# Experts of a product-key layer: the look-up of the chosen ones in PSUM, some splits on GpSimd, the gate through DRAM, weights moved by 96 bytes

## The chip, the cores and the metric

One core of a Trainium2 chip runs the whole kernel. Its engines are TensorE (PE, with PEld for its weight loads), VectorE (DVE), ScalarE (ACT), GpSimd (POOL) and SyncE (SP), which issues all DMAs. The metric is the device time of one execution in microseconds; the median over the runs is given.

## The reference

Two blocks of a transformer follow each other on 256 tokens of width 1024: two layers with feed-forward parts, convolution, pooling and neighbourhood attention, then one layer with retention, sparse attention and a mixture of experts. Only the experts and what frames them matter here:

```python
q = (hblk @ w_q).reshape(B, TB, 8, 2, 128)
s = jnp.einsum('btphd,phnd->btphn', q, subkeys)
v, i = lax.top_k(s, 16)
cand = (v[..., 0, :, None] + v[..., 1, None, :]).reshape(B, TB, 8, 256)
cidx = (i[..., 0, :, None] * 128 + i[..., 1, None, :]).reshape(B, TB, 8, 256)
tv, tj = lax.top_k(cand, 16)
eidx = jnp.take_along_axis(cidx, tj, axis=-1)
w = jax.nn.softmax(tv, axis=-1)
a = jax.nn.gelu(jnp.einsum('btd,btpkd->btpk', hblk, w_down[eidx]))
y = jnp.einsum('btpk,btpkd->btd', w * a, w_up[eidx])
x = x + ga2[:, None, :] * y      # then rms_norm(x, g_norm_final)
```

There are 128 x 128 = 16384 experts. Each token chooses 16 for each of 8 heads: the best 16 of 128 first keys, the best 16 of 128 second keys, and the best 16 of their 256 sums.

## The kernel before, in words

All matrices are float32. To keep that precision a weight `w` is split into a high part (`activation Copy` to float32r on ACT, L252) and the rest (`w - high`, on POOL at L254 or on DVE at L256); a product is then three matmuls (`mm3`, L298 to L300: high by high, high by low, low by high).

`Stream` (L232 to L285) feeds the weights in a fixed order of units of 128 x 1024. A unit is loaded by SP into a raw buffer, split into one of four buffers, and used. Splits run three units ahead of the use. The split buffers of the experts' stage are `hl0`, `hl1` and two parts of Hh and Hl called `c0`, `c1` (second half of each, L1153 to L1155); the raw ones are `raw0`, `raw1` and two parts of X. A pad of 56 floats (`gap0`) ahead of `hl0` puts hl at 224 bytes past a multiple of 256; units that `wide` names are put 8 floats further on:

```python
if hl.shape[-1] == SPLIT:
    o = 8 if wide(label) else 0
    hl = hl[:, o:o + 2048].rearrange("p (a n) -> p a n", a=2)
```

`c0` and `c1` begin at 2048 floats of Hh and Hl, at a multiple of 256 bytes, for all units alike.

The last third of the kernel is `peer`. It has these stages:

- 16 query units `wpq` and the key scores (L1611 to L1620), for 256 tokens in two halves of 128.
- All 16384 experts are computed for all tokens: `expert(e)` is one row of 128 experts, 24 matmuls of 256 columns with the weights `wdn` e as the stationary operand. Gelu on ACT (L1593) puts the 128 x 256 result into slot e. While the first rows run on PE, DVE computes the top-k (`topk`): sorts (L1750 to L1758), the sums (L1766), more sorts, and then the look-up, which finds the keys of the chosen pairs by comparing with a table of 0 to 15 (`iota`), multiplying and adding up (L1788, L1791, L1793, 2048 elements each, four times). Its scratch is `cand` in SBUF, its table is in SBUF, and DVE runs in program order, as every engine does.
- The result is transposed (L1648) into SELT. From then on, between the matmuls of the further rows, each token gets a 128 x 128 matrix of its weights: two one-hots on DVE (L1670 for four tokens, L1674 for one) and a product on PE (L1682). Four tokens fill one bank of PSUM, in turn banks 5, 6, 7; `place` multiplies them into the finished slots on DVE (L1691) and copies them to the others on ACT (L1693). The table is copied to bank 4 first (L1656). Experts rotate over banks 0 to 3 here and over six banks before.
- `finish`: for e from 0 to 127 slot e is split (`prep`, L324 and L325, two rows ahead, rows 0 and 1 after the last expert) and is the stationary operand for the weights `wup` e: 12 matmuls of 512 columns (L1841) added up in banks 4 to 7. After e = 32 `ends` loads the residual and the final norm's weights, and spreads the gate over the partitions: eight diagonal matrices on DVE (L1831), eight products with a matrix of ones on PE (L1832), two copies (L1833). The tail gates, adds, normalises and stores.

Of the kernel before, what the change touches and what calls it, by code (L numbers as in the profile page):

```python
# [189 lines left out]
class Stream:  # L190
# [45 lines left out]
    def split(self, upto):  # L236
        nc = self.nc
        while self.done < min(upto, len(self.units)):
            i = self.done
            self.load(i + 1)  # L240
            label, _, n, split = self.units[i]
            if i not in self.raws:
                return
            if split:
                hl = self.buf(i, 2)
                if hl is None:
                    return
                if hl.shape[-1] == SPLIT:
                    o = 8 if wide(label) else 0
                    hl = hl[:, o:o + 2048].rearrange("p (a n) -> p a n", a=2)  # L250
                raw = self.raws.pop(i)
                nc.scalar.activation(hl[:, 0, :n], raw[:, :n], AF.Copy)  # L252
                if i in (1, 2) or label[0] == "wdn" or (label[0] == "win2f" and label[1] > 7 or label[0] == "win2r" or label[:2] == ("winf", 1) and label[2] in (0, 4, 11) or label[0] == "wout2" and label[1] < 5):
                    nc.gpsimd.tensor_tensor(hl[:, 1, :n], raw[:, :n], hl[:, 0, :n].bitcast(F32), OP.subtract)  # L254
                else:
                    nc.vector.tensor_tensor(hl[:, 1, :n], raw[:, :n], hl[:, 0, :n].bitcast(F32), OP.subtract)  # L256
                self.hls[i] = hl
            self.done += 1
# [28 lines left out]
class Build:  # L287
# [40 lines left out]
    def run(self):  # L328
        nc, tc, ctx, I = self.nc, self.tc, self.ctx, self.I
        ctx.enter_context(tc.manual_schedule())  # L330
        base = ctx.enter_context(tc.tile_pool(name="base", bufs=1))
        psum = ctx.enter_context(tc.tile_pool(name="psum", bufs=1, space=bass.MemoryType.PSUM))
        self.bank = [psum.tile([P, 512], F32, name=f"bank{b}") for b in range(8)]
        self.X = base.tile([P, 2, KD, S], F32, name="X")
        self.Hh = base.tile([P, 2, KD, S], F32R, name="Hh")
        self.Hl = base.tile([P, 2, KD, S], F32R, name="Hl")
        raw = [base.tile([P, 1024], F32, name=f"raw{j}") for j in range(2)]
        base.tile([P, 56], F32, name="gap0")
        hl = [base.tile([P, SPLIT], F32R, name=f"hl{j}") for j in range(2)]
        self.con1 = base.tile([P, N1], F32, name="con1")  # L340
        self.mad2 = base.tile([P, 48], F32, name="mad2")
        self.half = base.tile([P, 4], F32, name="halfc")
        base.tile([P, 16], F32, name="gap1")
        self.sm = ctx.enter_context(tc.tile_pool(name="small", bufs=2))

        self.W = Stream(nc, 5, 3)
        self.plan()
        fb = ExitStack()
        fbp = fb.enter_context(tc.tile_pool(name="fb", bufs=1))
        self.G = fbp.tile([P, 2, 8, 512], F32R, name="G")  # L350
        self.Gh, self.Gl = self.G[:, 0], self.G[:, 1]
        self.raws = [("r0", raw[0]), ("r1", raw[1]), ("r2", fbp.tile([P, 1024], F32, name="raw2"))]
        fbp.tile([P, 56], F32, name="gap2")
        self.hls = [("h0", hl[0]), ("h1", hl[1])]
        self.hls += [(f"h{j}", fbp.tile([P, SPLIT], F32R, name=f"hl{j}")) for j in (2, 3)]
        W = self.W
        W.ring(0, self.raws, self.hls)

        cc = self.np_cc = base.tile([P, KD, 2], F32, name="cc")
        nc.sync.dma_start(cc.rearrange("p k c -> p (k c)"), I["cvt"])  # L360
        nc.sync.dma_start(self.con1, I["con1"])
        nc.vector.memset(self.half, -0.5)
        self.C = {k: self.con1[:, o:o + n] for k, (o, n) in OFF1.items()}
        self.ring = [0, 1, 2, 3, 4, 5]

        self.np = fb.enter_context(tc.tile_pool(name="norm", bufs=2))
        self.gn = self.np.tile([P, 72], F32, name="gn", bufs=1)
        nc.sync.dma_start(self.gn, I["gn"])
        with tc.tile_pool(name="mod", bufs=2) as mp:
            with tc.tile_pool(name="first", bufs=8) as self.fm:  # L370
                self.mods_setup(mp)
            self.first_block()
            self.need(2, 5)
        self.second_mix()
        self.peer(fb)
# [768 lines left out]
    def second_mix(self):  # L1144
        nc, tc, I, W = self.nc, self.tc, self.I, self.W
        T = S
        with tc.tile_pool(name="mix2", bufs=1) as p:
# [2 lines left out]
            W.ring(W.done, self.raws + [("xr", Xc[:, 1024:])], self.hls + [("hx", p.tile([P, SPLIT], F32R, name="hx"))])  # L1150
            W.ring(W.index("win2r", 0, 0), self.raws, self.hls + [("hx", W.rings[-1][2][-1][1])])
            Xf = self.X.rearrange("p a k t -> p a (k t)")
            Hf = [H[:, 1].rearrange("p k t -> p (k t)").rearrange("p (a n) -> p a n", a=2) for H in (self.Hh, self.Hl)]  # L1153
            W.ring(W.index("wpq", 4), self.raws[:2] + [("x0", Xf[:, 1, :1024]), ("x1", Xf[:, 1, 1024:])],
                   self.hls[:2] + [(f"c{j}", Hf[j]) for j in range(2)])  # L1155
            con = p.tile([P, N2 - P], F32, name="con2")
# [402 lines left out]
    def peer(self, fb):  # L1559
        nc, tc, I, W = self.nc, self.tc, self.I, self.W  # L1560
        T = S
        ident = self.C["ident"]
        xd = tc.dram_tile([P, 2 * D], F32, name="xd")
        Xf = self.X.rearrange("p a k t -> p a (k t)")
        fb.close()
        bs = self.pq
        pp = self.ctx.enter_context(tc.tile_pool(name="pp", bufs=1))
        SELT = Xf[:, 0, :768].rearrange("p (a t) -> p a t", a=3)
        con = pp.tile([P, P], F32, name="iota")
        self.SA = self.ctx.enter_context(tc.tile_pool(name="slota", bufs=1)).tile([P, NSA * S], F32, name="slotA")  # L1570
        slots = [self.SA[:, e * S:(e + 1) * S] for e in range(NSA)]
        built = [0]
# [26 lines left out]
        with tc.tile_pool(name="topk", bufs=1) as p:  # L1599
# [27 lines left out]
                scores(f, bs.pop(0))  # L1627
            nc.sync.dma_start(xd, xt.rearrange("p t d -> p (t d)"))
            nc.sync.dma_start(con, I["con2"][:, OFF2["iota"][0]:OFF2["iota"][0] + P])
            top = self.topk(p, con, SC, SEL)  # L1630
            e = 0
            spare = 0.0
            while spare is not None and e < NSA - 4:
# [17 lines left out]
                self.dump("SELT", Xf[:, 0, :1024])  # L1651
        slotB = self.ctx.enter_context(tc.tile_pool(name="slots", bufs=1)).tile([P, (P - 1 - NSA) * S], F32, name="slotB")
        slots += [slotB[:, j * S:(j + 1) * S] for j in range(P - 1 - NSA)] + [Xf[:, 0, 1792:2048]]
        self.ring = [0, 1, 2, 3]
        io = self.bank[4][:, :P]
        nc.vector.tensor_copy(io, con)  # L1656
        wb = [5, 6, 7]
        SAv = self.SA.rearrange("p (e t) -> p e t", t=S)
        SCv = Xf[:, 0:1, 1792:2048]
        SBv = slotB.rearrange("p (e t) -> p e t", t=S)  # L1660
# [16 lines left out]
        def weight(t):  # L1677
            if t >= T:
                return
            oh = ohs.pop(t)  # L1680
            o = self.bank[wb[t // 4 % 3]][:, t % 4 * P:(t % 4 + 1) * P]
            nc.tensor.matmul(o, firsts[t // 4][:, t % 4], oh, start=True, stop=True)  # L1682

        def place(g, e):

            bv = self.bank[wb[g % 3]].rearrange("p (t e) -> p e t", e=P)
            ts = slice(4 * g, 4 * g + 4)
            for v, e0, e1 in ((SAv, 0, NSA), (SBv, NSA, P - 1), (SCv, P - 1, P)):
                m = min(max(e, e0), e1)
                if m > e0:  # L1690
                    nc.vector.tensor_tensor(v[:, :m - e0, ts], v[:, :m - e0, ts], bv[:, e0:m], OP.mult)  # L1691
                if m < e1:
                    nc.scalar.activation(v[:, m - e0:, ts], bv[:, m:e1], AF.Copy)  # L1693
            built[0] = 4 * g + 4
# [16 lines left out]
                tok[0] += 1  # L1711

        rest = None
        while e < P or tok[0] < T:
            g0 = tok[0] // 4
            if e < P:
# [12 lines left out]
            if e < P:  # L1729
                rest = gelu(e, o)  # L1730
                e += 1
        if rest:
            rest()

        self.finish(slots, xd, pp)

    def topk(self, p, iota, SC, SEL):

# [43 lines left out]
        io = iota[:, :16].unsqueeze(1).broadcast_to((P, P, 16))  # L1782
        for a in range(2):
            for t in range(2):
                eq = cand[t]
                iv = i16f[t].rearrange("p (h a) n -> p h a n", a=2)
                flat = eq.rearrange("p h k n -> p (h k) n")
                nc.vector.tensor_tensor(flat, abf[t][:, a].rearrange("p h k -> p (h k)").unsqueeze(2).broadcast_to((P, P, 16)),  # L1788
# [14 lines left out]
            nc.vector.tensor_tensor(w[t], w[t], b16(ss[t][:, 1].unsqueeze(2)), OP.mult)  # L1803
        yield 1.2

    def finish(self, slots, xd, pp):
        nc, I, W = self.nc, self.I, self.W
        acc = [[self.bank[4 + 2 * t + c] for c in range(2)] for t in range(2)]
        cs = {}
        Hx = self.Hh[:, 0].rearrange("p k t -> p (k t)")  # L1810
        Hf4 = [Hx[:, j * 512:(j + 1) * 512] for j in range(4)]

        def prep(e):
            c = Hf4[e % 4].rearrange("p (a t) -> p a t", a=2)
            self.split2((c[:, 0], c[:, 1]), slots[e])
            cs[e] = c

        ga = self.mod(2, 0, 5)
        SA = self.SA
        xt = SA[:, :2048].rearrange("p (t d) -> p t d", t=2)  # L1820
        gf, gab, tmp = [SA[:, j * 1024:(j + 1) * 1024] for j in range(2, 5)]
        dgs = [SA[:, 5120 + j * P:5120 + (j + 1) * P] for j in range(4)]

        def ends():

            nc.sync.dma_start(SA[:, :2048], xd)
            nc.sync.dma_start(gf, I["gfin"].broadcast_to((P, D)))
            for n in range(2):
                b = self.bank[n]
                for j in range(4):  # L1830
                    nc.vector.tensor_scalar(dgs[j], self.C["ident"], ga[:, 4 * n + j:4 * n + j + 1], None, op0=OP.mult)  # L1831
                    nc.tensor.matmul(b[:, j * P:(j + 1) * P], self.C["ones"], dgs[j], start=True, stop=True)  # L1832
                nc.vector.tensor_copy(gab[:, n * 512:(n + 1) * 512], b)  # L1833

        def up(e, u, t, c, outer=False):
            ts = slice(t * P, (t + 1) * P)
# [5 lines left out]
                                 start=e == 0 and a + b == 0, stop=e == P - 1 and a == 1)  # L1842

        LATE = 4
        prep(0)
        prep(1)
        for e in range(P - LATE):
            u = W.next("wup", e)
# [44 lines left out]
```

## Time and profile before

| | us |
|---|---|
| median of 3 runs | 2723.25 (2722.06 to 2727.45) |
| profiled execution | 2724.21 |
| its span | 2722.3 |
| PE busy | 2639.4 (97%) |
| PEld, DVE, ACT, POOL busy | 2312.6, 1759.6, 1102.2, 507.7 |
| HBM read | 446.35 MB, 165 GB/s |

The span runs from the first to the last instruction; the execution's own time is 1.9 us more. Matmuls overlap, so the busy time of PE says where it stands still, and the distance between starts says how fast it is.

### The profile page before, as it was taken

To read this page: it belongs to the slowest core of one execution; us is meant where nothing else is said; L and a number is where in the kernel's file an instruction comes from. 1 tells how busy PE (TensorE), PEld (TensorE's weight loads), DVE (VectorE), ACT (ScalarE), POOL (GpSimd) and SP (SyncE) were. 2 spreads that over 40 slices of the span, in tenths; PEclk is the share of its full clock that TensorE was granted. 3 is DMA by queue.
4 is the path that set the end of the run, shared out by engine and by line. 5 is a ranking of instruction groups with operands and counts; after the bars stand their busy time and mean duration, and the time that the engine had idled before them with its cause. 6 is when DMAs were issued, how large, how long until landed. Compare 5 with 4: busy or idle time off the path is not lost. (4 is left out here: it accounts for less than half of the span.)

```text
span 2722.3 us, 40945 instructions
## 1 busy us (share of the span) xinstructions
PE 2639.4 (97%) x15899; PEld 2312.6 (85%) x15899; DVE 1759.6 (65%) x3389; ACT 1102.2 (40%) x1867; POOL 507.7 (19%) x284
## 2 busy tenths in 40 slices
PE   6999999999999999999998999989999999999998
PEld 4888888688888898888978999778999999988887
DVE  6877865557777565555546656775795566655555
ACT  5322234534222242222354445553444545454554
POOL 1000011120000010000122001332697666300000
PEclk9999999999999999999999999999999999999999
DMA  6655643234566535655344655524555444566664
GB/s 246 200 188 182 205 151 111 67 101 140 193 189 194 182 124 186 203 190 194 108 149 130 191 188 172 174 75 160 171 165 169 151 151 148 157 196 204 193 193 140
DMA packets 129476, 451.40 MB, mean 166 GB/s; under 512 B 16000, under 2 KB 21120, under 8 KB 127744
## 3 DMA queue, kind: packets, MB, share of 16 engines
q1 hardware_dynamic: 129280, 448.77, 51.4%
q8 instruction: 125, 2.05, 0.3%
q14 instruction: 71, 0.58, 0.1%
HBM read 446.35 MB, written 2.10 MB: 165 GB/s over the span
## 5 line engine op out<-in xcount | busy, mean ns | idle before, releaser
L298 PE MATMUL bank<-Hh,hl 128*128 128x256 f32 (+1 forms) x1968 | 661.4, 336 | 9.4 <-ACT Hh L661 5.1
L300 PE MATMUL bank<-Hh,hl 128*128 128x256 f32 (+1 forms) x1968 | 639.9, 325 | 4.1 <-POOL hl L254 4.1
L299 PE MATMUL bank<-Hl,hl 128*128 128x256 f32 (+1 forms) x1968 | 640.4, 325 | 0.8 <-DVE Hl L664 0.7
L252 ACT ACTIVATE hl<-raw 128x1024 fp32r<-128x1024 f32 (+1 forms) x401 | 410.9, 1041 | 276.4 <-DMA raw<-in_w_dram 84.1
L256 DVE TENSOR_TENSOR hl<-raw,hl 128x1024 fp32r<-128x1024 f32 (+1 forms) x316 | 383.1, 1222 | 180.2 <-ACT hl L252 177.2
L298 PEld LDWEIGHTS bank<-Hh,hl 128*128 128x128 f32 x1968 | 375.8, 191 | 48.5 <-issue 7.7
L300 PEld LDWEIGHTS bank<-Hh,hl 128*128 128x128 f32 x1968 | 375.2, 191 | 35.2 <-POOL hl L254 4.9
L299 PEld LDWEIGHTS bank<-Hl,hl 128*128 128x128 f32 x1968 | 375.8, 191 | 30.7 <-DVE Hl L664 1.8
L512 DVE SCALAR_TENSOR_TENSOR junk<-wm,cb 128x1024 bf16<-128x1024 f32 x272 | 332.1, 1221 | 11.0 <-ACT cb L518 7.6
L615 POOL TENSOR_TENSOR nacc<-nlast,nacc 128x256 f32<-128x256 f32 (+1 forms) x56 | 60.7, 1089 | 1320.3 <-issue 834.4
L254 POOL TENSOR_TENSOR hl<-raw,hl 128x1024 fp32r<-128x1024 f32 x85 | 212.8, 2507 | 163.1 <-ACT hl L252 157.7
L298 PE MATMUL bank<-G,hl 128*128 128x512 f32 (+1 forms) x673 | 227.6, 338 | 0.0
L300 PE MATMUL bank<-G,hl 128*128 128x512 f32 (+1 forms) x673 | 226.8, 337 | 0.0
L299 PE MATMUL bank<-G,hl 128*128 128x512 f32 (+1 forms) x673 | 226.8, 337 | 0.0
L324 ACT ACTIVATE G<-silu 128x512 fp32r<-128x512 f32 (+1 forms) x88 | 51.1, 580 | 407.1 <-DVE silu L801 407.1
L1841 PE MATMUL bank<-hl,Hh 128*128 128x512 f32 x768 | 179.5, 390 | 0.0
L801 DVE TENSOR_TENSOR silu<-silu,bank 128x512 f32<-128x512 f32 (+1 forms) x88 | 54.6, 621 | 189.1 <-PE bank L300 184.0
L298 PE MATMUL bank<-Hh,hm 128*128 128x512 f32 (+1 forms) x496 | 175.5, 354 | 0.0
L299 PE MATMUL bank<-Hl,hm 128*128 128x512 f32 (+1 forms) x496 | 175.3, 353 | 0.0
L300 PE MATMUL bank<-Hh,hm 128*128 128x512 f32 (+1 forms) x496 | 175.3, 353 | 0.0
L1841 PEld LDWEIGHTS bank<-hl,Hh 128*128 128x128 f32 x768 | 144.3, 188 | 29.8
L727 DVE SCALAR_TENSOR_TENSOR X<-bank,mall,X 128x256 f32<-128x256 f32 x192 | 84.5, 479 | 125.8 <-PE bank L300 125.7
(370 smaller groups left out, 5061.9 us busy)
## 6 DMA issues: line engine op xcount, KB each, us to landing
raw<-in_w_dram SPq DMA_DIRECT2D x208, 512.0 KB, 4.1
wm<-in_wmod_dram SPq DMA_DIRECT2D x128, 512.0 KB, 4.3
X<-in_wdn_dram SPq DMA_DIRECT2D x64, 512.0 KB, 3.6
raw<-in_wdn_dram SPq DMA_DIRECT2D x64, 512.0 KB, 3.6
X<-in_wup_dram SPq DMA_DIRECT2D x64, 512.0 KB, 3.6
raw<-in_wup_dram SPq DMA_DIRECT2D x64, 512.0 KB, 3.6
raw<-in_w_dram SPq DMA_DIRECT2D x64, 448.0 KB, 3.9
wm<-in_wada_dram SPq DMA_DIRECT2D x48, 512.0 KB, 4.6
```

What stands on the lines that cost most here:

```text
L252: nc.scalar.activation(hl[:, 0, :n], raw[:, :n], AF.Copy)
L254: nc.gpsimd.tensor_tensor(hl[:, 1, :n], raw[:, :n], hl[:, 0, :n].bitcast(F32), OP.subtract)
L256: nc.vector.tensor_tensor(hl[:, 1, :n], raw[:, :n], hl[:, 0, :n].bitcast(F32), OP.subtract)
L298: mm(o, wh, xh, start=start, stop=False)
L299: mm(o, wh, xl, start=False, stop=False)
L300: mm(o, wl, xh, start=False, stop=stop)
L324: nc.scalar.activation(dst[0], src, AF.Copy)
L512: nc.vector.scalar_tensor_tensor(junk, w, 1.0, self.cb[c], op0=OP.mult, op1=OP.mult, accum_out=o)
L615: self.nadd.tensor_tensor(acc, last, acc, OP.add)
L727: nc.vector.scalar_tensor_tensor(x, self.bank_(b, T, half), g[:, d:d + 1], x, op0=OP.mult, op1=OP.add)
L801: nc.vector.tensor_tensor(s, s, self.bank_(bb, T), OP.mult)
L1841: nc.tensor.matmul(acc[t][n], c[:, a, ts], u[:, b, n * 512:(n + 1) * 512], start=e == 0 and a + b == 0, stop=e == P - 1 and a == 1)
```

## The change

- Look-up: PSUM banks 4 to 7 become one tile, `four`, with the banks as slices. The look-up's scratch is `four`, its table is copied to bank 3 as soon as it is loaded, and from there on experts rotate over banks 0, 1, 2; the tokens' matrices use four banks, 4 to 7.
- The low parts of the `wup` units 0 to 3 are computed on GpSimd; before, on VectorE.
- Row 0 of the second product is split into a new tile (`zero`) as soon as all tokens' matrices are placed, before the last expert.
- The gate is written to DRAM (`gd`, 1024 numbers) at the start of `peer` and read back spread over the partitions in `ends`, without the diagonal products.
- Hh and Hl are 64 floats longer; `c0` and `c1` begin at 2104 floats, 96 bytes past a multiple of 128 (and 224 past one of 256).

```diff
-                if i in (1, 2) or label[0] == "wdn" or (label[0] == "win2f" and ...):
+                if i in (1, 2) or label[0] == "wdn" or label[0] == "wup" and label[1] < 4 or (label[0] == "win2f" and ...):
                     nc.gpsimd.tensor_tensor(hl[:, 1, :n], raw[:, :n], hl[:, 0, :n].bitcast(F32), OP.subtract)
...
-        self.bank = [psum.tile([P, 512], F32, name=f"bank{b}") for b in range(8)]
+        self.bank = [psum.tile([P, 512], F32, name=f"bank{b}") for b in range(4)]
+        self.four = psum.tile([P, 2048], F32, name="four")
+        self.bank += [self.four[:, b * 512:(b + 1) * 512] for b in range(4)]
         self.X = base.tile([P, 2, KD, S], F32, name="X")
-        self.Hh = base.tile([P, 2, KD, S], F32R, name="Hh")
-        self.Hl = base.tile([P, 2, KD, S], F32R, name="Hl")
+        self.Hs = [base.tile([P, 2 * KD * S + 64], F32R, name=n) for n in ("Hh", "Hl")]
+        self.Hh, self.Hl = [H[:, :2 * KD * S].rearrange("p (a k t) -> p a k t", a=2, k=KD) for H in self.Hs]
...
-            Hf = [H[:, 1].rearrange("p k t -> p (k t)").rearrange("p (a n) -> p a n", a=2) for H in (self.Hh, self.Hl)]
+            Hf = [H[:, 2104:4152].rearrange("p (a n) -> p a n", a=2) for H in self.Hs]
...
+        self.gd = tc.dram_tile([1, D], F32, name="gd")
+        nc.sync.dma_start(self.gd.rearrange("o (j p) -> p (o j)", p=P), self.mod(2, 0, 5))
...
+        zero = pp.tile([P, 512], F32R, name="zero")
...
-            top = self.topk(p, con, SC, SEL)
+            self.ring = [0, 1, 2]
+            io = self.bank[3][:, :P]
+            nc.vector.tensor_copy(io, con)
+            top = self.topk(p, io, SC, SEL)
...
-        self.ring = [0, 1, 2, 3]
-        io = self.bank[4][:, :P]
-        nc.vector.tensor_copy(io, con)
-        wb = [5, 6, 7]
+        wb = [4, 5, 6, 7]
...
+            if tok[0] == T and not early and rest:
+                early = [self.sides(zero, slots[0])]
...
-                eq = cand[t]
+                eq = self.four.rearrange("p (h k n) -> p h k n", h=8, k=16)
...
+    def sides(self, c, slot):
+
+        c = c.rearrange("p (a t) -> p a t", a=2)
+        self.split2((c[:, 0], c[:, 1]), slot)
+        return c
...
             nc.sync.dma_start(gf, I["gfin"].broadcast_to((P, D)))
-            for n in range(2):
-                b = self.bank[n]
-                for j in range(4):
-                    nc.vector.tensor_scalar(dgs[j], self.C["ident"], ga[:, 4 * n + j:4 * n + j + 1], None, op0=OP.mult)
-                    nc.tensor.matmul(b[:, j * P:(j + 1) * P], self.C["ones"], dgs[j], start=True, stop=True)
-                nc.vector.tensor_copy(gab[:, n * 512:(n + 1) * 512], b)
+            nc.sync.dma_start(gab, self.gd.broadcast_to((P, D)))
...
-        prep(0)
         prep(1)
```

## Rows read from the trace of the kernel before

**Rows 1.** Stretches: start:end, length, busy us of each engine (instructions), clock, DMA share, GB/s.
```profile
2100.00:2200.00 100.00, 100.00 (x859) 100.00 (x858) 57.61 (x171) 50.95 (x139) 68.15 (x29) 1.00 0.49 152
...
2352.00:2363.00 11.00, 8.59 (x64) 7.57 (x63) 7.66 (x19) 5.60 (x16) 0.00 (x0) 1.00 0.35 101
...
2448.00:2456.00 8.00, 6.80 (x37) 5.48 (x36) 5.51 (x15) 2.73 (x4) 0.00 (x0) 1.00 0.87 310
...
2600.00:2707.00 107.00, 107.00 (x473) 88.68 (x473) 61.19 (x79) 52.97 (x79) 0.00 (x0) 1.00 0.55 177
```

**Rows 2.** Waits of PE from 1926 to 2066: us in total, times, longest.
```profile
PE bank L300 <- POOL hl L254: 4.1, 4, 1.3
PE bank L300 <- POOL Hh L254: 1.3, 1, 1.3
```

**Rows 3.** Timeline of ACT, the first and last of 12 gelus: start, length, instruction.
```profile
2010.91 0.38 ACT L1593 ACTIVATE slotA<-bank 128x256 f32<-128x256 f32 x1 [1.54 <-PE bank L300]
...
2050.30 0.38 ACT L1593 ACTIVATE slotA<-bank 128x256 f32<-128x256 f32 x1 [0.99 <-PE bank L300]
```

**Rows 4.** Timelines of DVE and of POOL in the look-up.
```profile
2002.21 2.27 DVE L1788 TENSOR_TENSOR cand<-abf,iota 128x2048 f32<-128x2048 f32 x1
...
2022.31 4.51 DVE L1788 TENSOR_TENSOR cand<-abf,iota 128x2048 f32<-128x2048 f32 x1
...
2022.27 2.40 POOL L254 TENSOR_TENSOR Hl<-X,Hl 128x1024 fp32r<-128x1024 f32 x1
2024.63 8.82 POOL L254 TENSOR_TENSOR hl<-raw,hl 128x1024 fp32r<-128x1024 f32 x2
```

**Rows 5.** Timeline of PE: a wide unit at 1346 us, and four experts from 1990 us.
```profile
1346.11 0.28 PE L298 MATMUL bank<-Hh,hl 128*128 128x256 f32 x1
...
1348.99 0.28 PE L298 MATMUL bank<-Hh,hl 128*128 128x256 f32 x1
...
1990.87 0.28 PE L298 MATMUL bank<-Hh,hl 128*128 128x256 f32 x1
...
1996.47 0.28 PE L298 MATMUL bank<-Hh 128*128 128x256 f32 x1
...
1999.35 0.28 PE L298 MATMUL bank<-Hh,Hl 128*128 128x256 f32 x1
```

**Rows 6.** Timelines of PE and of DVE between the two products.
```profile
2355.21 0.28 PE L300 MATMUL bank<-Hh,hl 128*128 128x256 f32 x1
2356.93 0.49 PE L1682 MATMUL bank<-oh,X 128*128 128x128 f32 x2 [1.45 <-DVE oh L1674]
...
2361.01 1.20 PE L1841 MATMUL bank<-Hh 128*128 128x512 f32 x4 [0.78 <-ACT Hh L324]
...
2364.36 2.90 PE L1841 MATMUL bank<-Hl,Hh 128*128 128x512 f32 x12
...
2355.33 1.23 DVE L256 TENSOR_TENSOR Hl<-X,Hl 128x1024 fp32r<-128x1024 f32 x1 [1.73 <-ACT Hl L252]
```

**Rows 7.** Timeline of PE around the gate's products in the second product.
```profile
2448.70 2.88 PE L1841 MATMUL bank<-Hh 128*128 128x512 f32 x12
...
2454.85 3.01 PE L1841 MATMUL bank<-Hl,Hh 128*128 128x512 f32 x12
2457.70 2.66 PE L1841 MATMUL bank<-hl,Hh 128*128 128x512 f32 x11
```

**Rows 8.** Timeline of DVE at the transposes of the result.
```profile
2064.82 1.09 DVE L1649 COPY X<-bank 128x256 f32<-128x256 f32 x3 [15.34 <-PE bank L1648]
```

**Rows 9.** Timeline of SP's queue at the start of the experts' part.
```profile
1861.14 5.33 SPq L232 DMA_DIRECT2D raw<-in_wpq_dram  x2
1882.74 0.33 SPq L1608 DMA_DIRECT2D subk<-in_subk_dram  x1
```

**Rows 10.** Timelines of DVE and ACT, first and last instruction of one placing.
```profile
2343.66 0.43 DVE L1691 TENSOR_TENSOR slotA<-slotA,bank 128x272 f32<-128x272 f32 x1
...
2344.49 0.17 ACT L1693 ACTIVATE X<-bank 128x4 f32<-128x4 f32 x1
```

More of the change, by code (lines that the diff above doesn't have):

```diff
@@ L252, in split @@
                 nc.scalar.activation(hl[:, 0, :n], raw[:, :n], AF.Copy)
-                if i in (1, 2) or label[0] == "wdn" or (label[0] == "win2f" and label[1] > 7 or label[0] == "win2r" or label[:2] == ("winf", 1) and label[2] in (0, 4, 11) or label[0] == "wout2" and label[1] < 5):
+                if i in (1, 2) or label[0] == "wdn" or label[0] == "wup" and label[1] < 4 or (label[0] == "win2f" and label[1] > 7 or label[0] == "win2r" or label[:2] == ("winf", 1) and label[2] in (0, 4, 11) or label[0] == "wout2" and label[1] < 5):
                     nc.gpsimd.tensor_tensor(hl[:, 1, :n], raw[:, :n], hl[:, 0, :n].bitcast(F32), OP.subtract)
@@ L1680, in weight @@
             oh = ohs.pop(t)
-            o = self.bank[wb[t // 4 % 3]][:, t % 4 * P:(t % 4 + 1) * P]
+            o = self.bank[wb[t // 4 % 4]][:, t % 4 * P:(t % 4 + 1) * P]
             nc.tensor.matmul(o, firsts[t // 4][:, t % 4], oh, start=True, stop=True)
         def place(g, e):
-            bv = self.bank[wb[g % 3]].rearrange("p (t e) -> p e t", e=P)
+            bv = self.bank[wb[g % 4]].rearrange("p (t e) -> p e t", e=P)
             ts = slice(4 * g, 4 * g + 4)
@@ L1713, in peer @@
         rest = None
+        early = []
         while e < P or tok[0] < T:
@@ L1731, in peer @@
                 e += 1
+            if tok[0] == T and not early and rest:
+                early = [self.sides(zero, slots[0])]
         if rest:
             rest()
-        self.finish(slots, xd, pp)
+        self.finish(slots, xd, early)
     def topk(self, p, iota, SC, SEL):
@@ L1804, in topk, with finish @@
         yield 1.2
-    def finish(self, slots, xd, pp):
+    def sides(self, c, slot):
+        c = c.rearrange("p (a t) -> p a t", a=2)
+        self.split2((c[:, 0], c[:, 1]), slot)
+        return c
+    def finish(self, slots, xd, early):
         nc, I, W = self.nc, self.I, self.W
         acc = [[self.bank[4 + 2 * t + c] for c in range(2)] for t in range(2)]
-        cs = {}
+        cs = dict(enumerate(early))
         Hx = self.Hh[:, 0].rearrange("p k t -> p (k t)")
@@ L1813, in prep @@
         def prep(e):
[L1814 to L1818, printed above, removed]
+            cs[e] = self.sides(Hf4[e % 4], slots[e])
         SA = self.SA
@@ L1821, in finish @@
         gf, gab, tmp = [SA[:, j * 1024:(j + 1) * 1024] for j in range(2, 5)]
-        dgs = [SA[:, 5120 + j * P:5120 + (j + 1) * P] for j in range(4)]
         def ends():
```

## Prediction

> **What bounds the kernel now.** I read the page's 40 slices first: PE is busy in nearly all of them, so time can only be won where PE stands still or where its matmuls follow each other too slowly. The diff touches the last third alone (experts, 1883 us to the end), so I cut that part into stretches [rows 1]. In the routing stretch 2100 to 2200 and in the second product 2600 to 2707 PE is full: 100 of 100 us and 107 of 107. The reader is to see there that a faster DVE or POOL gives nothing, and that the only price is the distance between matmuls: 473 in 107.00 us, 0.226 us each with 512 columns. Three places are not full: the look-up at the end of the top-k (2010 to 2050), the seam between the two products (2352 to 2363, 8.59 of 11) and the gate in the second product (2448 to 2456, 6.80 of 8). I then asked for PE's waits in the look-up [rows 2], the times of both engines concerned [rows 3, 4], and single matmuls at the other places [rows 5 to 7].
>
> **Look-up in PSUM (term A).** PE waits there for POOL's splits of the weights, and POOL waits for DVE. ACT's gelu follows each expert, so its starts show the pace: 11 experts from 2010.91 to 2050.30 took 39.39 us [rows 3]. Undisturbed, two experts with weights in hl take 5.60 us and one in Hh 2.88 us [rows 5], 2.84 us on average, 31.2 us for 11. So 8.1 us are lost; the two largest of PE's recorded waits alone are 5.4 us [rows 2], which leave out the slow restart after each stop. The reason is in [rows 4]: L1788 takes 2.27 us when it starts first, but 4.51 us when a split of 2.40 us started just ahead of it, and the next two splits then took 8.82 us in place of 4.8. The two engines exclude each other, instruction by instruction, while DVE reads two operands in SBUF. The change puts the table (iota, bank 3) and the scratch (banks 4 to 7) in PSUM; then each look-up instruction reads one operand in SBUF. That DVE ops with one PSUM operand leave POOL alone is seen in the routing stretch: POOL is busy 68.15 us with 29 splits, 2.35 us each, while DVE runs its PSUM-fed one-hots [rows 1]. What a 2048-element DVE instruction from PSUM to PSUM costs has no row. From below it is the 2.27 us, from above the 4.51 us of now; even at the upper price nothing is lost, since DVE idles 15.34 us before the result is fetched [rows 8]. I take 8.1 us, bounds 5.4 and 8.1. Two things are new on this path. Iota's copy moves to DVE ahead of the top-k, inside the same idle 15 us. And experts now rotate over three banks, not six, so the last of the three transposes at 2064 goes into the bank that was just read by gelu (0.38 us, [rows 3]): 0.3 us lost, and the copy of iota that no longer stands between transposes and one-hots gives back as much. I count both as zero.
>
> **Weight offset 96 (term B).** Half of the experts' weights are split into Hh and Hl at a multiple of 128 bytes, the others into hl, which lies 96 bytes behind one. [rows 5] has both in one expert stage: 48 matmuls from hl in 5.60 us (0.1167 each), 24 from Hh in 2.88 (0.1200). It is the address and not the tile: at 1346 us hl itself, moved by 8 floats to a multiple of 128 for the "wide" units, also takes 2.88 us for 24. The change moves the weights in Hh and Hl to 2104 floats, 96 bytes behind a multiple of 128. 64 of 128 experts win 0.08 us: 5.1 us; of the 12 wpq units in this ring half win the same, 0.5. B is 5.6 us; PE is full there, so all of it counts. Against it stands the second product, which uses the same buffers as the 512-column moving operand. All its matmuls now start at a multiple of 128, and no row shows another offset at that width. The nearest rows give the bound: 3.3 ns per matmul either way, 64 experts of 12 matmuls, 2.5 us lost or won, twice that if the width doubles it. I take zero: at 512 columns nothing in the rows says which way.
>
> **Seam: splits on GpSimd, first row split early (term C).** At 2355.21 the last matmul of expert 126 starts, and the next waits until 2356.93 for a one-hot, which stands on DVE behind the split at 2355.33 (1.23 us) [rows 6]. Then expert 127 ends, and the second product starts only at 2361.01, after gelu and the split of row 0; its second rank-128 update starts at 2364.36. From 2355.21 to 2364.36 are 9.15 us. The work in it is 25 matmuls of 0.117, 12 of 0.226 and two short ones, about 0.2: 5.85 us. So 3.3 us are lost. With the first four splits on POOL, idle there (0.00 in 2352 to 2363 [rows 1]), DVE is free for the one-hots, and row 0 is split while expert 127 runs. What could be late next is row 1, whose low half is needed four matmuls into its own update, 3.6 us after expert 127. Its DVE instruction (two operands in SBUF) can meet a POOL split and wait up to 2.40 us [rows 4]; gelu (0.38) and the ACT steps ahead of it leave it about as much. I take 3.2 us, bounds 0.8 and 3.3. The Trainium skill (SBUF — State Buffer, Who interferes with whom) says that DVE instructions with two SBUF inputs and GpSimd instructions that read SBUF lock each other out for a whole instruction. By that rule the splits put on GpSimd bring the lock into the seam, where today no POOL work runs; [rows 4] agree with the rule, and the rival below prices it.
>
> **Gate through DRAM (term D).** At 2448.70 an update starts, the one after next at 2457.70 [rows 7]: 9.00 us for 24 matmuls of 0.226, 5.4 us. 3.5 us go into eight diagonal products and their waits for DVE. The change loads the spread gate as 512 KB more behind the two loads that are there. At the 310 GB/s of this stretch [rows 1] that delays the weights behind it by 1.7 us. A split is asked for three experts ahead, three times 2.7 us, and needs some 2.4 us, so 5 us cover it; without the cover it would cost those 1.7 us. Writing the gate is 1024 pieces of four bytes on SP's queue, behind the loads of wpq and ahead of the load of subk. SP is idle there from 1866.47 to 1882.74, 16.3 us [rows 9]; eight times the 0.33 us of a load with 128 pieces is 2.6 us. It costs nothing. D is 3.5 us.
>
> **Sum.** 8.1 + 5.6 + 3.2 + 3.5 = 20.4 us, against the profiled execution's 2724.21 us (span 2722.3): 2703.8. That execution lies 0.96 us above the median 2723.25, so the median should come to 2702.9.
>
> **Rivals.**
> 1. The second product slows at offset 96: 768 matmuls at 3.3 to 6.6 ns, 2.5 to 5 us given back, 2705 to 2708. For it: the code moves hl by 8 floats for this very width. Against it: nothing measured. 0.20.
> 2. The look-up still holds POOL, or another wait (the weights' DMA, ACT's table loads for the softmax) shows behind the one removed: A falls to 0 to 4 us, 2707 to 2711. For it: ACT has also waits for DMA in this stretch. Against it: those come from POOL's late release of buffers, and outside the stretch the same DMA load leaves PE full. 0.10.
> 3. The lock moves to the seam: row 1's low half waits 2.40 us behind a POOL split; 2705.3. 0.09.
> 4. Slower than before: banks 4 to 7 are now one tile. If one-hot products into one bank had to wait for the placing of another bank, each of the 64 groups would hold PE for about as long as placing takes, 2343.66 to 2344.66, 1.0 us [rows 10]: 64 us, less 20: about 2767. It decides from 0.32 us a group. Against it: parts of X are used in the same way today (one-hots, weights and SELT in one tile) with PE full. 0.04.
> 5. The offset does nothing in the experts (B is zero, as if the tile were the cause): 2708.5. 0.05.
>
> **How the numbers follow.** The forecast, all four terms as summed, has the chance 0.52, with a range of its own from 2701 to 2706. From 2698 (second product faster by 2.5, and small gains) to 2711 rivals 1, 2, 3 and 5 are in; outside lie rival 4 and mishaps together, some 0.1. A change under 0.2%, 5.4 us, can't be told from none here. Only several rivals at once reach above 2717.8: 0.03 for the same, 0.04 for slower, 0.93 for faster. Predicted: 2703 us.
>
> **What would show it.** A: L1788 and L1791 at 2.3 us each time, POOL splits at 2.4 throughout, no wait of PE for POOL from 1926 to 2066. B: all experts at 2.80 us. C: no gap over 0.3 us between expert 126 and the second update. D: no gap at update 33. Updates alternating between 2.72 us and more would show rival 1. It is wrong if PE waits anew in the seam or among the groups of the routing.

## The result, and the profile after

The changed kernel takes 2902.77 us, the median of six runs (2900.5 to 2905.59); the kernel before took 2723.64 in six runs beside them (2722.06 to 2727.45). The ratio is 1.0658, with a 95% interval from 1.0647 to 1.0669. The forecast was 2703 us and faster; the kernel became 179 us slower.

The stretches of the trace show where. The first fence is the kernel before, the second the changed kernel, both cut at the same points of the program: start, load of subk (the experts' part begins), first transpose of the look-up's result, first matmul of the second product, end. The columns are start:end, length, busy us of PE, PEld, DVE, ACT and POOL (with instructions), clock, DMA share, GB/s.

```profile
0.00:1882.70 1882.70, 1820.09 (x10385) 1557.28 (x10386) 1229.85 (x2157) 696.80 (x1092) 177.86 (x154) 0.99 0.51 163
1882.70:2064.30 181.60, 174.24 (x1455) 171.88 (x1454) 139.44 (x436) 83.07 (x123) 135.14 (x48) 1.00 0.58 180
2064.30:2361.00 296.70, 293.89 (x2512) 293.26 (x2510) 182.08 (x517) 146.74 (x392) 192.88 (x81) 1.00 0.48 150
2361.00:2722.30 361.30, 351.15 (x1552) 290.15 (x1552) 208.21 (x280) 175.65 (x262) 1.86 (x2) 0.99 0.58 185
```

```profile
0.00:2045.20 2045.20, 1876.41 (x10385) 1598.12 (x10386) 1225.81 (x2157) 698.30 (x1092) 176.84 (x154) 0.96 0.47 150
2045.20:2221.40 176.20, 171.43 (x1455) 170.34 (x1454) 134.32 (x437) 81.69 (x123) 117.91 (x48) 0.99 0.60 187
2221.40:2535.60 314.20, 300.34 (x2513) 293.00 (x2511) 177.12 (x514) 141.44 (x390) 197.11 (x83) 1.00 0.45 140
2535.60:2903.80 368.20, 356.21 (x1536) 289.36 (x1536) 207.95 (x268) 176.77 (x264) 6.81 (x4) 0.99 0.56 184
```

The first row carries nearly everything: 162.5 us are lost ahead of the experts, in code in which the diff moves no operation, with the same 10385 matmuls. The look-up's stretch is 5.4 us shorter, the routing's 17.5 us longer, the second product's 6.9 us longer: 162.5 - 5.4 + 17.5 + 6.9 = 181.5, the difference of the spans. The last three differences mix the loss with what the change wins in these stretches; the run reopened, below, takes the two apart.

PE's waits ahead of the experts say what it waits for (line waited for: us in total, times, longest). First the kernel before, then the changed one:

```profile
PE bank L623 <- DVE nacc L615: 17.2, 1, 17.2
PE bank L298 <- ACT Hh L661: 5.1, 4, 1.8
```

```profile
PE four L298 <- DVE ht L661: 38.6, 13, 6.1
PE four L1112 <- ACT pt L1099: 23.5, 22, 3.2
PE four L625 <- DVE nacc L617: 17.1, 1, 17.1
```

All rows of this view together are 61.9 us before and 168.6 us after. The wait of 17 us for nacc is in both. Nearly all of the others that are new are PE waiting to write into `four` for a DVE or ACT instruction that reads `four`. One of them, on PE, on DVE, and in stretches (same columns as above):

```profile
428.57 0.28 PE L300 MATMUL bank<-Hh,hl 128*128 128x256 f32 x1
434.11 0.58 PE L298 MATMUL four<-Hh,hl 128*128 128x256 f32 x1 [5.25 <-DVE ht L661]
434.48 0.41 PE L299 MATMUL four<-Hl,hl 128*128 128x256 f32 x1
434.70 0.41 PE L300 MATMUL four<-Hh,hl 128*128 128x256 f32 x1
```

```profile
428.18 0.87 DVE L661 SCALAR_TENSOR_TENSOR ht<-X,mall,four 128x256 f32<-128x256 f32 x2 [3.27 <-PE four L645]
...
433.57 0.48 DVE L661 SCALAR_TENSOR_TENSOR ht<-X,mall,four 128x256 f32<-128x256 f32 x1
```

```profile
427.00:428.90 1.90, 1.85 (x16) 1.65 (x15) 0.72 (x2) 0.21 (x1) 0.00 (x0) 1.00 0.00 0
428.90:434.10 5.20, 0.00 (x0) 0.00 (x0) 5.01 (x14) 3.26 (x8) 0.00 (x0) 0.89 0.00 0
434.10:436.00 1.90, 1.90 (x9) 1.90 (x10) 1.26 (x3) 1.44 (x2) 0.00 (x0) 0.50 0.00 0
```

`chunk` (L661) normalises the next block; it reads the row statistics, which lie in bank 7, a slice of `four`. The product of L298 accumulates in another bank of `four`. It starts at 434.11, just after the last of the eight readers of bank 7 ends (433.57 + 0.48 = 434.05). Then comes a second price: after these 5.2 us without a matmul the granted clock is 0.50 (the 1.2 GHz level), and matmuls follow each other at 0.22 us in place of 0.12.

The two prices can be told apart in the stretch ahead of the experts. The waits there grew by 107 us (168.6 - 61.9). The other 56 us lie in PE's busy time: the same 10385 matmuls keep it busy for 1876.41 us in place of 1820.09. The clock is enough to explain them. Over the whole span its mean is 0.968 after and 0.991 before; with the two levels 1.00 and 0.50 this is 2 x 0.032 x 2903.8 = 186 us at the lower one against 2 x 0.009 x 2722.3 = 49 us, 137 us more, and at half speed 137 us of matmuls cost at most 68 us. This is an estimate, since part of the time at the lower level falls into the waits themselves.

In the routing stretch the same thing happens on a smaller scale, here between two products, and in the list of waits:

```profile
2521.03 0.28 PE L300 MATMUL bank<-Hh 128*128 128x256 f32 x1
2521.77 0.49 PE L1687 MATMUL four<-oh,X 128*128 128x128 f32 x2 [0.46 <-ACT X L1698]
```

```profile
PE four L1687 <- ACT X L1698: 12.7, 30, 0.5
```

The product of a token's one-hots waits until ACT has copied another group's result (L1698). From 2521.03 to 2521.77 are 0.74 us where 0.12 would do, so 0.62 are lost; 30 times this is 18.6. Without the single tile the stretch takes 290.9 us (the run reopened), so the loss in it is 23.3 us, of which these waits are the greater part. The compiled program carries them. Its list of PE's instructions in order, for products in the middle of a group (two of the kernel before, then one of the changed kernel):

```
11833 L1682 MATMUL bank_69<-oh,X 128x128 [waits DVE_49]
11840 L1682 MATMUL bank_69<-oh,X 128x128 [waits DVE_49]

11835 L1687 MATMUL four<-oh,X 128x128 [waits DVE_49,Activation_49]
```

Before, only the first product into a bank waits for ACT.

What was forecast for the four terms is in the trace as well. The look-up runs at one speed, and POOL's splits beside it do so too (compare [rows 4], 4.51 and 8.82 us); DVE, then POOL:

```profile
2194.64 2.29 DVE L1796 TENSOR_TENSOR four<-abf,bank 128x2048 f32<-128x2048 f32 x1
```

```profile
2193.87 2.41 POOL L254 TENSOR_TENSOR Hl<-X,Hl 128x1024 fp32r<-128x1024 f32 x1 [0.23 <-ACT Hl L252]
2196.23 4.79 POOL L254 TENSOR_TENSOR hl<-raw,hl 128x1024 fp32r<-128x1024 f32 x2
```

And PE at the seam (compare [rows 6]) and further into the second product (compare [rows 7]):

```profile
2535.30 0.27 PE L300 MATMUL bank<-Hh,hl 128*128 128x256 f32 x1
2535.58 3.06 PE L1846 MATMUL four<-Hh,zero 128*128 128x512 f32 x12
2538.47 2.96 PE L1846 MATMUL four<-Hl,Hh 128*128 128x512 f32 x12
...
2618.74 5.63 PE L1846 MATMUL four<-hl,Hh 128*128 128x512 f32 x24
2624.20 2.96 PE L1846 MATMUL four<-Hh 128*128 128x512 f32 x12
2627.00 2.96 PE L1846 MATMUL four<-Hl,Hh 128*128 128x512 f32 x12
```

The seam has no gap over 0.3 us. But 12 matmuls from Hh or Hl now take 2.80 us (2624.20 to 2627.00, 0.233 each), those from hl 2.73 (2618.74 to 2624.20 for 24): this is rival 1.

### The profile page after: what moved, and what is told of

It reads as the page before. It is cut to its first block, busy times and chain, and to the rows that moved or that the text cites. A ratio compares the mean times of both kernels' runs of the same rounds, so it can differ in the third digit from the quotient of the medians.

```text
span 2903.8 us, 40994 instructions
## 1 busy us (share of the span) xinstructions
PE 2704.4 (93%) x15883; PEld 2350.8 (81%) x15883; DVE 1745.2 (60%) x3375; ACT 1098.2 (38%) x1867; POOL 498.7 (17%) x288
## 5 line engine op out<-in xcount | busy, mean ns | idle before, releaser
L298 PE MATMUL bank<-Hh,hl 128*128 128x256 f32 (+1 forms) x1720 | 587.8, 342 | 9.1 <-ACT Hh L663 7.3
L300 PE MATMUL bank<-Hh,hl 128*128 128x256 f32 (+1 forms) x1720 | 564.1, 328 | 0.0
L298 PEld LDWEIGHTS bank<-Hh,hl 128*128 128x128 f32 x1720 | 337.4, 196 | 44.6 <-issue 9.7
L300 PEld LDWEIGHTS bank<-Hh,hl 128*128 128x128 f32 x1720 | 336.8, 196 | 26.0
L1846 PE MATMUL four<-hl,Hh 128*128 128x512 f32 x768 | 180.2, 390 | 0.0
L1846 PEld LDWEIGHTS four<-hl,Hh 128*128 128x128 f32 x768 | 144.2, 188 | 31.1
L298 PE MATMUL bank<-G,hl 128*128 128x512 f32 (+1 forms) x492 | 169.2, 344 | 0.0
L299 PE MATMUL bank<-G,hl 128*128 128x512 f32 (+1 forms) x492 | 168.3, 342 | 0.0
L300 PE MATMUL bank<-G,hl 128*128 128x512 f32 (+1 forms) x492 | 168.3, 342 | 0.0
L298 PE MATMUL four<-Hh,hm 128*128 128x512 f32 (+1 forms) x312 | 113.4, 363 | 19.5 <-DVE ht L661 19.5
L256 DVE TENSOR_TENSOR hm<-raw,hm 128x1024 fp32r<-128x1024 f32 (+1 forms) x95 | 113.2, 1202 | 11.6 <-ACT hm L252 11.3
L252 ACT ACTIVATE hm<-raw 128x1024 fp32r<-128x1024 f32 (+1 forms) x95 | 95.1, 1024 | 63.8 <-DMA raw<-in_w_dram 51.9
L1687 PE MATMUL four<-oh,X 128*128 128x128 f32 x512 | 101.5, 279 | 13.8 <-ACT X L1698 12.7
L299 PE MATMUL four<-Hl,hm 128*128 128x512 f32 (+1 forms) x312 | 112.5, 361 | 0.0
```

The costliest lines, as they stand in the source:

```text
L298: mm(o, wh, xh, start=start, stop=False)
L299: mm(o, wh, xl, start=False, stop=False)
L300: mm(o, wl, xh, start=False, stop=stop)
L1846: nc.tensor.matmul(acc[t][n], c[:, a, ts], u[:, b, n * 512:(n + 1) * 512], start=e == 0 and a + b == 0, stop=e == P - 1 and a == 1)
```

## Experiments

Two theories stood against each other for the loss. Theory 1: the tile. PSUM banks 4 to 7 are slices of one tile, and the program's waits are made for whole tiles, so a writer of one bank waits for the readers of all four, everywhere in the kernel. Theory 2: the memory layout. Hh and Hl are longer, which shifts what lies behind them, and the new offset slows matmuls.

**one_tile.** The kernel before with the four banks as one tile, and nothing else. The look-up stays in SBUF.

```diff
-        self.bank = [psum.tile([P, 512], F32, name=f"bank{b}") for b in range(8)]
+        self.bank = [psum.tile([P, 512], F32, name=f"bank{b}") for b in range(4)]
+        self.four = psum.tile([P, 2048], F32, name="four")
+        self.bank += [self.four[:, b * 512:(b + 1) * 512] for b in range(4)]
```

> The kernel before with one edit: banks 4 to 7 are slices of one tile. Theory 1 (waits between banks): whoever writes one of the four banks waits for readers of the others, in the whole kernel; 2885 to 2915 us, and PE's waits ahead of the experts rise by more than 100 us. Theory 2 (addresses): the longer Hh and Hl shift all later buffers and slow the matmuls; then this kernel stays at 2723.

Measured: 2997.86 us (2995.76 to 2999.61), ratio 1.1005 (1.0986 to 1.1023). The largest waits of PE:

```profile
PE four L1684 <- DVE oh L1676: 64.7, 91, 4.1
PE four L298 <- DVE ht L661: 39.2, 14, 6.1
```

Its routing stretch:

```profile
2234.20:2631.60 397.40, 329.42 (x2513) 309.80 (x2511) 198.97 (x517) 142.61 (x392) 191.66 (x81) 0.99 0.36 112
```

The tile alone makes the kernel slower than the whole change does. The loss ahead of the experts is the same (39.2 us of the wait for L661, against 38.6 above; all waits of PE there 166.5 us against 168.6). The time lies 83 us above the expected range, and the routing stretch is 83 us longer than in the changed kernel (397.4 against 314.2). Here the table that every one-hot reads is in bank 4, in the same tile as the tokens' matrices in banks 5 to 7, and products wait 91 times for a one-hot (L1676). In the changed kernel that table is in bank 3, outside the tile.

**off96.** The kernel before with the longer Hh and Hl and the weights at 2104 floats.

```diff
-        self.Hh = base.tile([P, 2, KD, S], F32R, name="Hh")
-        self.Hl = base.tile([P, 2, KD, S], F32R, name="Hl")
+        self.Hs = [base.tile([P, 2 * KD * S + 64], F32R, name=n) for n in ("Hh", "Hl")]
...
+            Hf = [H[:, 2104:4152].rearrange("p (a n) -> p a n", a=2) for H in self.Hs]
```

> The kernel before with only Hh and Hl 64 floats longer and their weight buffers at 2104 floats. Theory 1: 2717 to 2724: the experts win 5.6 us, and the second product, whose matmuls from Hh and Hl stand 7 ns further apart in the changed kernel, gives back some 5. Theory 2: 2850 or more.

Measured: 2722.54 us (2721.34 to 2730.17), ratio 1.0 (0.9991 to 1.001). Theory 2 falls. The last three stretches, cut at the same points:

```profile
1880.80:2059.50 178.70, 171.60 (x1455) 169.62 (x1454) 148.39 (x436) 82.47 (x123) 131.24 (x47) 1.00 0.57 181
2059.50:2353.40 293.90, 290.98 (x2512) 290.35 (x2510) 182.24 (x517) 147.02 (x392) 195.17 (x82) 1.00 0.48 153
2353.40:2720.50 367.10, 356.95 (x1552) 290.00 (x1552) 208.50 (x280) 175.49 (x262) 1.85 (x2) 0.99 0.55 182
```

Both expert stretches win, 2.9 and 2.8 us, together 5.7. The second product gives 5.8 back. That the time stays the same here means two changes that cancel.

**reopened.** The changed kernel, but banks 4 to 7 are four tiles, except while the look-up runs. For the look-up their pool is closed and opened again with one tile of four banks, and afterwards closed and opened with four tiles.

```diff
+    def upper_banks(self):
+        self.upper.close()
+        pool = self.upper.enter_context(self.tc.tile_pool(name="upper", bufs=1, space=bass.MemoryType.PSUM))
+        self.bank[4:] = [pool.tile([P, 512], F32, name=f"bank{b}") for b in range(4, 8)]
+    def upper_four(self):
+        self.upper.close()
+        pool = self.upper.enter_context(self.tc.tile_pool(name="upper", bufs=1, space=bass.MemoryType.PSUM))
+        self.four = pool.tile([P, 2048], F32, name="four")
```

> The changed kernel, but banks 4 to 7 are four tiles again; the tile of four banks lives only for the look-up. Theory 1: 2703 to 2712, which is the predicted sum with up to 7 us given back by the second product, and PE waits for nobody's reading of another bank. Theory 2: about 2900, as the changed kernel.

Measured: 2709.79 us (2708.59 to 2712.18), ratio 0.9952 (0.9936 to 0.9969). The same work on the same banks is 193 us faster than the changed kernel. This settles the loss: it is the declaration of the tile, and not what is done with the banks. Its stretches, cut at the same points:

```profile
0.00:1881.60 1881.60, 1820.07 (x10385) 1556.77 (x10386) 1229.31 (x2157) 697.28 (x1092) 178.01 (x154) 0.99 0.50 163
1881.60:2052.50 170.90, 169.85 (x1454) 169.09 (x1453) 134.35 (x437) 81.61 (x123) 117.71 (x48) 1.00 0.62 193
2052.50:2343.40 290.90, 290.86 (x2513) 290.34 (x2512) 179.79 (x515) 146.49 (x390) 197.61 (x83) 1.00 0.50 152
2343.40:2706.90 363.50, 354.32 (x1538) 288.26 (x1536) 207.28 (x266) 176.01 (x264) 6.81 (x4) 0.99 0.56 186
```

Against these rows the single tile costs 163.6 us ahead of the experts, 5.3 in the look-up's stretch, 23.3 in the routing and 4.7 in the second product, where DVE reads `four` in the tail; together this is 196.9 us, the difference of the spans. PE's waits ahead of the experts add up to 60.9 us, as before (61.9), and those behind to 1.0 us, where the changed kernel has 20.7. The Trainium skill (PSUM — Partial Sum Buffer, PSUM bank collisions raise a hardware error) asks for PSUM to be guarded by bank and quadrant, or simply by bank. It asks this for the sake of right results and names no time. What this run adds is the price: with waits made for each bank the new waits of PE are gone, and with waits made for four banks at once the kernel takes 193 us more.

**reopened_wide.** The same, with the `wup` units in Hh and Hl put 8 floats further on, as those in hl are, so that they begin at a multiple of 128 bytes.

```diff
-                if hl.shape[-1] == SPLIT:
+                if len(hl.shape) == 2:
...
-            Hf = [H[:, 2104:4152].rearrange("p (a n) -> p a n", a=2) for H in self.Hs]
+            Hf = [H[:, 2104:4160] for H in self.Hs]
```

> As the run reopened, but the units of the second product start at a multiple of 256 bytes again, 8 floats behind offset 2104. If the offset slows the 512-column matmuls: 5 us below reopened and 0.227 us between all of them. If the single tile of four banks is what slowed them: the same time as reopened.

Measured: 2704.03 us (2702.14 to 2706.7), ratio 0.9932 (0.9915 to 0.9948). It is the fastest version of all. Three of its four stretches, and PE from the last matmuls of the experts on:

```profile
0.00:1880.70 1880.70, 1818.08 (x10385) 1555.01 (x10386) 1229.96 (x2157) 696.47 (x1092) 178.50 (x154) 0.99 0.50 163
...
2051.70:2342.60 290.90, 290.86 (x2513) 290.34 (x2512) 179.82 (x515) 146.52 (x390) 197.52 (x83) 1.00 0.48 152
2342.60:2700.20 357.60, 348.32 (x1538) 288.09 (x1536) 206.87 (x266) 176.12 (x263) 6.79 (x4) 0.99 0.58 189
```

```profile
2339.44 0.28 PE L300 MATMUL bank<-Hh,hl 128*128 128x256 f32 x1
...
2342.59 2.89 PE L1861 MATMUL bank<-Hh,zero 128*128 128x512 f32 x12
2345.32 2.88 PE L1861 MATMUL bank<-Hl,Hh 128*128 128x512 f32 x12
...
2429.64 2.88 PE L1861 MATMUL bank<-Hh 128*128 128x512 f32 x12
...
2435.08 5.60 PE L1861 MATMUL bank<-hl,Hh 128*128 128x512 f32 x24
```

The routing stretch is full (290.86 of 290.90 us), and every 12 matmuls of the second product take 2.72 us, whatever their buffer. Its last stretch is 5.9 us shorter than that of reopened (357.6 against 363.5).

**two_tiles.** The dose of theory 1 halved: the kernel before with banks 4 and 5 as one tile, 6 and 7 as another.

```diff
+        pairs = [psum.tile([P, 1024], F32, name=f"pair{b}") for b in range(2)]
+        self.bank += [pairs[b // 2][:, b % 2 * 512:(b % 2 + 1) * 512] for b in range(4)]
```

> The kernel before with banks 4 and 5 as slices of one tile and banks 6 and 7 as slices of another. Theory 1 (a write to one bank of a tile waits for readers of its other banks): part of the 275 us of the run with one tile of four stays, since only the partner bank is waited for; 2770 to 2920 us. If a tile of more than one bank costs something by itself (its address, its size), whoever shares it: as much as with one tile, 2980 to 3010.

Measured: 2800.09 us in two runs (2795.81 to 2804.37), ratio 1.0281 (1.0262 to 1.0299). The loss is 75 us (2800.09 - 2724.64, the kernel before beside it), against 275 for one tile of four (2997.86 - 2723.06). The wait for the one-hots is the one that falls most, now that only the groups in bank 5 share a tile with the table:

```profile
PE pair L1684 <- DVE oh L1676: 11.3, 19, 4.4
```

The wait for L661, 39.2 us with one tile of four, is no longer in the list: bank 7, which L661 reads, shares its tile with bank 6 alone.

**lookup.** The kernel before with the look-up in PSUM alone, its pool reopened as above.

> The kernel before with the look-up in PSUM alone, the tile of four banks living for the look-up only. Term A: 8 us faster, 2713 to 2717, no wait of PE for POOL in the top-k. Rival (another wait behind the one removed): 2719 or more.

Measured: 2714.7 us (2712.73 to 2715.82), ratio 0.9966 (0.9953 to 0.9979). From the load of subk to the first transpose of the result are 173.2 us where they were 181.6, so 8.4 us are won there (SP, then PE):

```profile
1882.52 0.33 SPq L1622 DMA_DIRECT2D subk<-in_subk_dram  x1
```

```profile
2055.72 1.07 PE L1666 MATMUL bank<-con,SEL 128*128 128x128 f32 x6
```

**seam.** The kernel before with the first four low parts on GpSimd and row 0 split early, as in the change's diff.

> The kernel before with the first four splits of the second product on GpSimd and row 0 split early, nothing else. Term C: 3.2 us less from the last matmul of expert 126 to the second update, 2719 to 2721. Rival (the lock moves to the seam): 0.8 us less, and a gap of about 2 us at row 1's low half.

Measured: 2719.99 us (2718.23 to 2723.92), ratio 0.9986 (0.9977 to 0.9995). From the last matmul of expert 126 to the second update are 5.87 us, and no gap is left between them:

```profile
2354.38 0.28 PE L300 MATMUL bank<-Hh,hl 128*128 128x256 f32 x1
...
2360.25 2.88 PE L1849 MATMUL bank<-Hl,Hh 128*128 128x512 f32 x12
```

**gate.** The kernel before with the gate through DRAM, as in the change's diff.

> The kernel before with the gate through DRAM alone. Term D: 3.5 us less, 2719 to 2720, updates 33 to 35 without a gap. Rival (the weights behind the larger load come late): a gap of up to 1.7 us within the next 20 us.

Measured: 2720.94 us (2718.14 to 2726.76), ratio 0.9988 (0.9979 to 0.9997). Where the diagonal products stood, updates now follow each other without a gap, and the list of PE's waits has none from there to 2700 us, so the rival's late weights do not show:

```profile
2447.34 2.88 PE L1838 MATMUL bank<-Hh 128*128 128x512 f32 x12
...
2452.78 5.60 PE L1838 MATMUL bank<-hl,Hh 128*128 128x512 f32 x24
```

## Why the prediction was wrong

**The step that failed** is the sentence "The diff touches the last third alone". It moves operations there alone, but `self.bank` belongs to the whole kernel: the ring of the products, the row statistics and the attention use banks 4 to 7 from the start. So the first two thirds were never looked at, and 162.5 of the 181.5 us were lost in them. The second step that failed, for a small part, is the zero for the second product in term B: it loses 5.8 us.

**Rival 4 had the right mechanism, with the wrong place, price and chance.** It was priced at the 64 groups of the routing, 1.0 us each. There it cost 23.3 us, most of it in some 30 waits that lose about 0.6 us each; so the sign that the prediction names last, new waits of PE among the groups, is there. Ahead of the experts the tile costs seven times as much (163.6 us): in the example the reader that PE waits for is not one copy but a row of them (eight readings at L661, of which the fence shows the first two and the last), and the clock falls behind the wait. What stood against the rival, that slices of X are used side by side with PE full, did not carry over to `four`. In the kernel before the products in the middle of a group wait for DVE alone, although ACT writes to another part of X in this stage (L1693, [rows 10]). So these parts of X, a tile in SBUF, are not guarded against each other there, and the four banks in one PSUM tile are. Why the two are treated differently stays open. The limit "from 0.32 us a group" was put to the routing alone; at 23.3 us for 64 groups the loss there is 0.36 us a group, just over it, and the rest of the kernel was put to no such test.

**Term A, 8.1 us.** It is right: 8.4 us in lookup, a little over its upper bound, and PE waits for POOL no more (rival 2 is out). In the changed kernel its stretch is only 5.4 us shorter, since the tile takes 5.3 us there; in reopened it is 10.7 us shorter, with some 2.9 us of term B in it. The instructions cost 2.28 to 2.30 us from PSUM to PSUM, near the lower bound of 2.27 us, and POOL's splits stay at 2.4 us.

**Term B, 5.6 us.** It is right in the experts: 5.7 us in off96 (rival 5 is out). The zero for the second product was wrong, and rival 1 is true: at 96 bytes a matmul of 512 columns takes 0.233 us in place of 0.227. The bound from above, 6.6 ns a matmul and 5 us, was met by the units in Hh and Hl (12 matmuls take 2.80 us in place of 2.72, so 64 units give 5.1 us); the units in hl, next to them, lose some 0.01 us each as well, and together 5.8 us were measured. By itself the offset is worth nothing, and with the units of the second product put back the kernel is 5.8 us faster by medians (2709.79 - 2704.03).

**Term C, 3.2 us.** It is right. From the last matmul of expert 126 to the second update are 5.87 us in seam and 5.88 in reopened_wide (2339.44 to 2345.32), where they were 9.15 [rows 6]: 3.3 us. Neither the 2.40 us of rival 3 nor any other gap shows there.

**Term D, 3.5 us.** It is right. Two updates take 5.44 us in gate (2447.34 to 2452.78), where they were 9.00 [rows 7]: 3.56 us. The writing of the gate in 1024 pieces shows nowhere: the load of subk, which stands behind it in SP's queue, comes at 1880.70 in reopened_wide, no later than before (1882.70).

The sum of the terms as forecast was 20.4 us. With the two flaws mended, reopened_wide wins 19.0 us by medians (2723.06 - 2704.03) and 22.1 by spans. The forecast of 2703 us is nearly the time of that kernel, not of this one, and that kernel lacks both the single tile and the offset in the second product. Lookup, seam and gate run alone give 9.9, 4.7 and 3.7 us by medians, and with 5.6 for term B that would be 24 us; each ratio has an interval of 2.5 to 3.5 us to either side, so the terms are better measured in their stretches, as above.

## What to carry to other kernels

When a change touches a buffer's declaration, look for every user of the buffer in the whole program, not only for the lines that the diff moves. In this kernel a tile that holds several PSUM banks makes a writer of one bank wait for readers of the others, and a stage that needs them as one can have its own tile for just that time. A change of an address that helps one product should be measured in each product that reads there, by the distance between its matmuls.

## What the runs showed of the hardware that was not expected

The start address of a unit acts in opposite directions in the two products. As stationary weights with 256 columns moving, a matmul takes 0.1167 us at 96 bytes past a multiple of 128 and 0.1200 at a multiple [rows 5]; as the moving operand of 512 columns it takes 0.233 us at the one and 0.227 at the other. Only these two offsets were compared. What the text ahead of the prediction calls a multiple of 256 is one of 128 only: in the compiled program Hh and Hl begin 128 bytes past a multiple of 256.

A wait of PE costs more than its length: behind the 5.2 us of the example the granted clock was 0.50, and matmuls stood 0.22 us apart in place of 0.12. The waits of at most 0.5 us in the routing left it at 1.00 in the row of that stretch.
